# A two-layer decoder trunk: weight buffers split into three pools, and feed-forward inputs scaled before their norm is known

## The chip, the cores and the metric

The kernel runs on one core of one Trainium2 chip. The metric is the time of the whole program in device microseconds (us), from launch to the last output; lower is better. The engines that matter are TensorE (PE in the profile, with its weight loads as PEld), VectorE (DVE), ScalarE (ACT), GpSimd (POOL) and SyncE (SP), which issues the loads of the weights. Each engine works off its own instructions in the order in which they were written for it; a scheduler chose that order when the program was built.

## What is computed

Two decoder layers over 256 tokens of width 2048, in float32. Each layer has a mixer (attention of several kinds, not touched by the change) and a gated feed-forward block of width 5632, with a norm before and after each:

```python
def rms_norm(x, w):
    y = x * rsqrt(mean(x * x, axis=-1) + 1e-6)
    return y * w
...
for layer in range(2):
    u = rms_norm(h, mix_norm_pre[layer])
    u = mixer(u)                                  # two input maps, attention, output map w_out
    h = h + rms_norm(u, mix_norm_post[layer])
    u = rms_norm(h, ffn_norm_pre[layer])
    u = (silu(u @ w_gate[layer]) * (u @ w_up[layer])) @ w_down[layer]
    h = h + rms_norm(u, ffn_norm_post[layer])
```

## The kernel before, in words

The 256 tokens are two tiles of 128 rows, t = 0 and t = 1. The program has six phases in a row: input map with attention, output map and feed-forward block of layer 0, then the same three of layer 1. A phase is a list of chunks (512 output columns each), and a chunk is a list of steps. A step loads one piece of weights, 256 rows by 512 columns (512 KB), and runs its matmuls for both token tiles.

Float32 accuracy comes from splitting. `split` writes a rounded part with ACT (line 222) and the remainder with DVE (line 223); each product is then three matmuls (lines 280 to 282 in an ordinary step, 304 to 306 in a fast one). Activations are split the same way after a transpose (line 384 makes the four transposes of a 128x512 tile).

In the feed-forward block most gate and up chunks are fast chunks (`FastChunk`): five ordinary steps, then three fast steps, which multiply 2x2 blocks with seven products in place of eight. A fast step needs four sums of weight blocks, which DVE forms from the loaded piece in three instructions (lines 266, 267, 268: `split_sums`), before one ACT and one DVE instruction split seven blocks at once (128x1792). Activations need sums of their own, made once per block in `sums_of_tiles`. The order of chunks is gate 0, up 0, gate 1, up 1, gate 2, then four down chunks, then again four fast chunks (up 2, gate 3, up 3, gate 4), four down chunks, and so on. So twelve fast steps follow each other with twenty ordinary ones between them; the texts call that a burst.

Weights live in one list of 13 places of 128x2048 (`self.wp`, 8 KB per partition each). An ordinary step takes one place for its two split parts and half a place for the loaded piece; a fast step takes two places for the parts and one for the loaded piece with its sums. `load_until` records loads ahead of the matmuls. It takes the place that has been free longest, whatever it held last, and stops when too few places are free (`SPARE` = 3, in feed-forward phases `SPARE_FFN` = 5). A transfer into a place waits, on the queue of SP, until whatever last used the place is done: a split on DVE, or matmuls on PE.

At the end of the output map (`end_out`), `post_residual` does the following for each token tile. The sum of squares of the map's output gives a factor `prf` (`rms`: one DVE instruction, a power on POOL, two more on DVE); four instructions add the scaled output to x (line 466); four ACT squares of the new x (line 446) and a second `rms` give the factor `pr` of the next norm (line 416); four instructions multiply x by `pr` and the norm's weights (line 479); then come the transposes and splits that the first feed-forward matmuls read. Tile 1 runs eight steps behind tile 0 near such a boundary, so its last matmuls run while tile 0 goes through this. At the end of the feed-forward block (`end_ffn`) the weighted x is transposed without the factor, which is multiplied in later, where the attention reads its results.

## Time and profile before

| what | value |
|---|---|
| median of 3 runs (range) | 2485.02 us (2480.92 to 2485.55) |
| profiled execution: time / span | 2482.63 us / 2480.9 us |
| mean granted clock of TensorE, of full speed | 0.985 |
| busy: PE / DVE / ACT / POOL | 2395.2 / 1752.4 / 1222.8 / 206.2 us |
| moved from memory | 453.67 MB, mean 183 GB/s |

The span is from the first to the last instruction of the profiled execution; what lies around it is 1.7 us. A busy PE counts overlapping matmuls once, so the span less the busy time is time in which PE did nothing. The granted clock falls to half (1.2 of 2.4 GHz) for a while after some pauses of PE; a share of 0.83 over 10 us means that it stood at half for a third of them.

### The profile page before, as it was taken

The page shows a single profiled execution, that of the slowest core. Times are in us where ns is not written, and L with a number is a line of the kernel's source. Part 1 is how long each engine was busy: PE and PEld are TensorE (multiplying, and loading weights), DVE is VectorE, ACT ScalarE, POOL GpSimd, SP SyncE. Part 2 cuts the span into 40 slices and gives each one's busy share as a digit, 9 for nine tenths or more (in the row PEclk, how much of TensorE's full clock was granted, in tenths as well). Part 3 has the DMA queues.
Part 4 walks back from the last instruction along what each step waited for, and adds up shares of the span by engine and source line. Part 5 has one row for each costly group of instructions (what it writes and reads, how often), then busy time and mean ns, then how long its engine had stood idle before and what let it go on. Part 6 is the DMA issues. An engine that isn't in the chain of part 4 may idle for free.

```text
span 2480.9 us, 32443 instructions
## 1 busy us (share of the span) xinstructions
PE 2395.2 (97%) x12235; PEld 2005.1 (81%) x12235; DVE 1752.4 (71%) x2669; ACT 1222.8 (49%) x1833; POOL 206.2 (8%) x265
## 2 busy tenths in 40 slices
PE   9999999899999999999999999999999999999998
PEld 7878877778888887888877888887878888888876
DVE  7865775577868787778776555566776868687775
ACT  6654563454545444445455544454454535444443
POOL 0330360200000000000121000101000000000011
PEclk9999999999999999999999999999999999999999
DMA  6533434454545645555575444554464645555563
GB/s 235 196 136 136 153 136 149 152 192 163 199 165 187 212 162 197 185 212 178 204 259 186 160 168 181 206 205 166 158 229 161 215 156 204 186 186 180 189 245 126
DMA packets 131133, 453.67 MB, mean 183 GB/s; under 512 B 15568, under 2 KB 20944, under 8 KB 130976
## 3 DMA queue, kind: packets, MB, share of 16 engines
q1 hardware_dynamic: 120704, 423.81, 48.5%
q0 software_dynamic: 8112, 26.52, 3.3%
q8 instruction: 96, 1.57, 0.3%
q10 hardware_dynamic: 2160, 1.27, 0.2%
q14 instruction: 61, 0.50, 0.1%
HBM read 443.11 MB, written 8.42 MB: 182 GB/s over the span
## 4 chain that ended last, share of the span: by engine, by line
PE 65%; DVE 8%; DMA 8%; ACT 3%; issue 2%; POOL 0%; SPq 0%; DVEq 0%; POOLq 0%; ACTq 0%
PE acc L280 9%; PE p L281 9%; PE p L282 9%; PE p L280 9%; PE acc L281 9%; PE acc L282 9%; DVE w L223 4%; DMA w<-in_ffn_w_gate 4%; DMA w<-in_ffn_w_up 3%; ACT w L222 2%; PE acc L305 1%; PE acc L306 1%; PE p L305 1%; PE acc L304 1%; PE p L306 1%
## 5 line engine op out<-in xcount | busy, mean ns | idle before, releaser
L223 DVE TENSOR_TENSOR w<-w,w 128x512 fp32r<-128x512 f32 (+3 forms) x1104 | 1112.7, 1040 | 482.1 <-ACT w L222 479.7
L222 ACT ACTIVATE w<-w 128x512 fp32r<-128x512 f32 (+3 forms) x1104 | 944.4, 892 | 929.0 <-DVE w L268 287.6
L280 PE MATMUL acc<-w,m 128*128 128x512 f32 (+2 forms) x1582 | 622.3, 396 | 16.3 <-ACT w L222 9.0
L281 PE MATMUL acc<-w,m 128*128 128x512 f32 (+2 forms) x1582 | 622.0, 394 | 0.0
L282 PE MATMUL acc<-w,m 128*128 128x512 f32 (+2 forms) x1582 | 621.5, 394 | 0.2 <-DVE m L226 0.2
L280 PE MATMUL p<-w,m 128*128 128x512 f32 x1146 | 454.2, 399 | 10.7 <-ACT w L222 8.7
L281 PE MATMUL p<-w,m 128*128 128x512 f32 x1146 | 455.3, 397 | 0.9 <-DVE w L223 0.8
L282 PE MATMUL p<-w,m 128*128 128x512 f32 x1146 | 454.9, 398 | 0.0
L280 PEld LDWEIGHTS acc<-w,m 128*128 128x128 f32 x1582 | 299.5, 190 | 82.5 <-ACT w L222 10.2
L282 PEld LDWEIGHTS acc<-w,m 128*128 128x128 f32 x1582 | 298.8, 189 | 66.6 <-DVE m L226 0.6
L281 PEld LDWEIGHTS acc<-w,m 128*128 128x128 f32 x1582 | 299.0, 189 | 65.6 <-DVE w L223 0.6
L280 PEld LDWEIGHTS p<-w,m 128*128 128x128 f32 x1146 | 216.0, 189 | 60.7 <-ACT w L222 10.7
L281 PEld LDWEIGHTS p<-w,m 128*128 128x128 f32 x1146 | 216.0, 188 | 51.2 <-DVE w L223 2.4
L282 PEld LDWEIGHTS p<-w,m 128*128 128x128 f32 x1146 | 216.0, 189 | 49.8 <-DVE m L223 0.2
L266 DVE TENSOR_TENSOR w<-w 128x512 f32<-128x512 f32 x126 | 86.8, 689 | 91.0 <-DMA w<-in_ffn_w_up 54.8
L305 PE MATMUL acc<-w,m 128*128 128x256 f32 x462 | 130.9, 285 | 5.3 <-DVE w L223 5.3
L304 PE MATMUL acc<-w,m 128*128 128x256 f32 x462 | 128.1, 284 | 6.8 <-ACT w L222 6.7
L306 PE MATMUL acc<-w,m 128*128 128x256 f32 x462 | 130.3, 284 | 0.0
L433 POOL DMA_DIRECT2D m<-in_ffn_norm_post x16 | 8.8, 551 | 1342.0 <-PE acc L282 663.1
L305 PE MATMUL p<-w,m 128*128 128x256 f32 x420 | 118.3, 284 | 1.3 <-DVE w L223 1.3
L306 PE MATMUL p<-w,m 128*128 128x256 f32 x420 | 117.7, 282 | 0.0
L304 PE MATMUL p<-w,m 128*128 128x256 f32 x420 | 114.4, 282 | 3.0 <-ACT w L222 3.0
(268 smaller groups left out, 2115.3 us busy)
## 6 DMA issues: line engine op xcount, KB each, us to landing
w<-in_ffn_w_gate SPq DMA_DIRECT2D x176, 512.0 KB, 4.1
w<-in_ffn_w_up SPq DMA_DIRECT2D x176, 512.0 KB, 3.8
w<-in_ffn_w_down SPq DMA_DIRECT2D x176, 512.0 KB, 4.7
w<-in_ev_w_in SPq DMA_DIRECT2D x104, 512.0 KB, 4.4
w<-in_od_w_in SPq DMA_DIRECT2D x96, 512.0 KB, 4.3
w<-in_ev_w_out SPq DMA_DIRECT2D x32, 512.0 KB, 4.6
w<-in_od_w_out SPq DMA_DIRECT2D x32, 512.0 KB, 4.5
xd<-m POOLq DMA_DIRECT2D x24, 256.0 KB, 4.1
```

The lines of the kernel that those rows point to most:

```text
L222: self.nc.scalar.activation(h, src, AF.Copy)
L223: self.nc.vector.tensor_sub(l, src, h.bitcast(F32))
L266: nc.vector.tensor_sub(b[:, 4:6], b[:, 0:1].broadcast_to([P, 2, 256]), b[:, 1:3])
L280: nc.tensor.matmul(acc, xh, s.wh[:, j], start=(s.first and j == 0), stop=False)
L281: nc.tensor.matmul(acc, xh, s.wl[:, j], start=False, stop=False)
L282: nc.tensor.matmul(acc, xl, s.wh[:, j], start=False, stop=end)
L304: nc.tensor.matmul(acc, xh, s.wh[:, b], start=s.first and i in (0, 2), stop=True, **kw)
L305: nc.tensor.matmul(acc, xh, s.wl[:, b], start=False, stop=True, **kw)
L306: nc.tensor.matmul(acc, xl, s.wh[:, b], start=False, stop=True, **kw)
L433: self.nc.gpsimd.dma_start(out=w, in_=src.broadcast_to([P, 512]))
```

## The change

The 13 places become three pools of the same total size: `WB` = 10 buffers for split weights (`wpool`, 80 KB per partition), `RAW` = 4 for loaded pieces (`rpool`, 16 KB) and two for the sums (`spool`, 8 KB). Each pool hands out its buffers in turn. Loads are recorded ahead as long as the steps from the current one on need no more than ten buffers. The seven blocks of a fast step are split in two parts: three blocks straight from the loaded piece, four from the sums.

The input of the feed-forward block is multiplied by a number that is known before the residual is added: `scale`, the inverse root of the sum of the mean square of x before the mixer (`v`, kept from the earlier norm) and the mean square of three quarters of the mixer's post-norm weights. The true factor divided by `scale` (`r`) is multiplied in later: by ACT in the silu, by DVE in the product of gate and up. `prenorm_factor` now runs after `post_residual` at both kinds of boundary, at ordinary priority, in `end_out` behind the activation sums too.

```diff
-        wpool = pool("w", bufs=1)
+        self.wpool = pool("w", bufs=WB)
+        self.rpool = pool("raw", bufs=RAW)
+        self.spool = pool("sums", bufs=2)
...
     def load_until(self, n, end=None):
...
-            if len(self.wp.free) < need + (self.spare - 1 - held if self.loaded > n else 0):
+            if sum(a.places for a in self.steps[n:self.loaded + 1]) > WB:
                 break
-            s.w = [self.wp.pop(1) for i in range(s.places)]
+            raw = self.rpool.tile([P, 1024], F32, name="raw", tag="raw")
+            w = [self.wpool.tile([P, 2048], F32R, name="w", tag="w") for i in range(s.places)]
...
     def split_sums(self, b, s, wh, wl):
-        nc.vector.tensor_sub(b[:, 4:6], b[:, 0:1].broadcast_to([P, 2, 256]), b[:, 1:3])
-        nc.vector.tensor_sub(b[:, 6], b[:, 1], b[:, 5])
-        nc.vector.tensor_sub(b[:, 7], b[:, 3], b[:, 6])
...
-        self.split(s.wh, s.wl, b[:, 1:8])
+        t = self.spool.tile([P, 1024], F32, name="sums", tag="sums").rearrange("p (b n) -> p b n", b=4)
+        nc.vector.tensor_sub(t[:, 0:2], b[:, 0:1].broadcast_to([P, 2, 256]), b[:, 1:3])
+        nc.vector.tensor_sub(t[:, 2], b[:, 1], t[:, 1])
+        nc.vector.tensor_sub(t[:, 3], b[:, 3], t[:, 2])
+        self.split(s.wh[:, :3], s.wl[:, :3], b[:, 1:4])
+        self.split(s.wh[:, 3:], s.wl[:, 3:], t)
...
-    def prenorm_factor(self, t):
+    def prenorm_factor(self, t, scaled=False):
...
+        if scaled:
+            self.nc.vector.scalar_tensor_tensor(self.r[t], y, f, self.unscale[t], op0=ALU.mult, op1=ALU.mult)
+        else:
+            self.nc.vector.tensor_mul(self.r[t], y, f)
...
+    def next_scale(self, t):
+        nc = self.nc
+        a, j, b = self.t("psa", [P, 1]), self.t("psj", [P, 3]), self.t("psb", [P, 1])
+        nc.vector.tensor_scalar(j, self.wss[:, :3], 1.0 / 1536, 0.0, op0=ALU.mult, op1=ALU.add, accum_out=a)
+        nc.vector.tensor_add(b, a, self.v[t])
+        y, f = self.rsqrt(b, 1, "ps")
+        self.scale[t], self.unscale[t] = self.t("pscale", [P, 1]), self.t("punscale", [P, 1])
+        nc.vector.tensor_mul(self.scale[t], y, f)
+        nc.vector.tensor_mul(self.unscale[t], b, self.scale[t])
...
+            elif then == "ffn":
+                nc.vector.scalar_tensor_tensor(y, x, self.scale[t], self.nwb[c], op0=ALU.mult, op1=ALU.mult)
+                self.aT[t].append(self.transposed(y))
...
-        if then != "out":
-            self.prenorm_factor(t)
-        if then == "ffn":
-            for c in range(4):
-                y = self.y[t][c]
-                nc.vector.scalar_tensor_tensor(y, self.x[t][c], self.r[t], self.nwb[c], op0=ALU.mult, op1=ALU.mult)
-                self.aT[t].append(self.transposed(y))
...
     def gate_fast(self, out):
-            self.nc.scalar.activation(a, a, AF.Silu)
+            self.nc.scalar.activation(a, a, AF.Silu, scale=self.r[t])
...
     def up_fast(self, f, out):
-            self.nc.vector.tensor_mul(u, out[t], u)
+            self.nc.vector.scalar_tensor_tensor(u, out[t], self.r[t], u, op0=ALU.mult, op1=ALU.mult)
...
     def out_chunk(self, t, layer, c, acc):
         self.norm_weight(y, "mix_norm_post", layer, c)
+        if t == 0:
+            if c == 0:
+                self.wss = self.t("wss", [P, 4], 2)
+            self.square_sum(y, self.wss[:, c:c + 1])
+        if c == 2:
+            self.next_scale(t)
...
     def end_out(self, t, layer):
         with self.tc.high_priority(offset=LEAD):
             self.post_residual(t, "ffn")
+        if t == 1:
+            self.sums_of_tiles(self.y)
+            for b in range(2):
+                self.mem.give(*self.y[b])
+        self.prenorm_factor(t, True)
```

The change moves instructions on every engine. Three places are shown, each as the built programs have it; line numbers of the changed program are its own. The first is the queue of SP in the feed-forward block of layer 0, where the loads of up 1 and gate 2 are issued; in brackets stand the semaphores that a row waits for (DMAHW: an earlier transfer; DVE, PE, Activation: that engine). Before:

```order
L247 DMA w_5538<-in_ffn_w_up 128x1024 [waits DMAHW6_49,DMAHW3_49,DVE_49]
L247 DMA w_5538<-in_ffn_w_up 128x1024
L257 DMA w_5662<-in_ffn_w_up 128x1024 [waits PE_49]
L257 DMA w_5629<-in_ffn_w_up 128x1024 [waits PE_49]
L257 DMA w_5606<-in_ffn_w_up 128x1024 [waits DMAHW4_49,DMAHW7_49,DMAHW3_49,DVE_49]
L247 DMA w_5698<-in_ffn_w_gate 128x1024 [waits DMAHW0_49,PE_49]
L247 DMA w_5698<-in_ffn_w_gate 128x1024 [waits DMAHW1_49]
L247 DMA w_5730<-in_ffn_w_gate 128x1024 [waits DMAHW2_49,PE_49]
L247 DMA w_5730<-in_ffn_w_gate 128x1024
```

And in the changed program:

```order
L248 DMA raw<-in_ffn_w_up 128x1024 [waits DMAHW0_49,DVE_49]
L248 DMA raw<-in_ffn_w_up 128x1024 [waits DMAHW1_49,DVE_49]
L248 DMA raw<-in_ffn_w_up 128x1024 [waits DMAHW2_49,DVE_49]
L241 DMA raw<-in_ffn_w_gate 128x1024 [waits DMAHW3_49,DVE_49]
L241 DMA raw<-in_ffn_w_gate 128x1024 [waits DMAHW4_49,DVE_49]
L241 DMA raw<-in_ffn_w_gate 128x1024 [waits DMAHW5_49,DVE_49,Activation_49]
L241 DMA raw<-in_ffn_w_gate 128x1024 [waits DMAHW7_49,DVE_49]
L241 DMA raw<-in_ffn_w_gate 128x1024 [waits DMAHW6_49,DVE_49]
```

Of the 808 loads of weights, 372 wait for PE before; in the changed program none does, and they come in the order of the steps.

The second place is ACT in the same burst: the splits of up 1's fast steps (`128x1792` before; `raw 128x768` and `sums 128x1024` now) among ordinary ones. Before:

```order
L222 ACTIVATE w_5660<-w_5662 128x1792 [waits DMAHW5_49,DVE_49,PE_49]
L686 ACTIVATE m_5594<-m_5594 128x512 [waits DVE_49]
L222 ACTIVATE w_5697<-w_5698 128x1024 [waits DMAHW0_49,PE_49]
L222 ACTIVATE w_5627<-w_5629 128x1792 [waits DMAHW6_49,DVE_49]
L222 ACTIVATE w_5604<-w_5606 128x1792 [waits DMAHW7_49,DVE_49]
L222 ACTIVATE w_5734<-w_5730 128x1024 [waits DMAHW3_49,PE_49]
L222 ACTIVATE w_5669<-w_5568 128x1024 [waits DMAHW2_49,DVE_49]
L222 ACTIVATE w_5729<-w_5730 128x1024 [waits DMAHW2_49,DVE_49]
L222 ACTIVATE w_5702<-w_5698 128x1024 [waits DMAHW1_49,DVE_49]
```

And in the changed program, where L301 is the chunk's first read of its results (L310 before) and L683 the silu (L686 before):

```order
L221 ACTIVATE w<-raw 128x768 [waits DMAHW4_49,PE_49,Activation_49]
L221 ACTIVATE w<-raw 128x768 [waits DMAHW5_49,PE_49,Activation_49]
L301 ACTIVATE m_5753<-p_5671 128x256 [waits PE_49]
L221 ACTIVATE w<-sums 128x1024 [waits DVE_49]
L221 ACTIVATE w<-raw 128x768 [waits DMAHW6_49,PE_49,Activation_49]
L221 ACTIVATE w<-sums 128x1024 [waits DVE_49]
L221 ACTIVATE w<-raw 128x1024 [waits DMAHW7_49,PE_49]
L683 ACTIVATE m_5753<-m_5753,pr 128x512 [waits DVE_49,Activation_49]
L221 ACTIVATE w<-raw 128x1024 [waits DMAHW0_49,PE_49]
L683 ACTIVATE m_5754<-m_5754,pr 128x512 [waits DVE_49]
L221 ACTIVATE w<-sums 128x1024 [waits DVE_49]
```

The wait for PE has moved from the load to the split. Before, two pieces of the next chunk (w_5697, w_5734) stand ahead of pieces that PE needs sooner (w_5604, w_5669); now the loaded pieces stand in the order of the steps, and the part from the sums follows a few rows behind.

The third place is DVE at the end of layer 0's output map, token tile 0: residual, factor and scaled input. Before (L466 residual, L416 the factor `pr`, L479 the scaled input, L223 remainders of weight splits):

```order
L466 SCALAR_TENSOR_TENSOR m_4260<-m_4788,prf,m_4260 128x512
L206 TENSOR_SCALAR pj,pv<-xss 128x5
L223 TENSOR_TENSOR w_4903<-w_4904,w_4903 128x512 x2
L223 TENSOR_TENSOR w_4916<-w_4904,w_4916 128x512
L195 SCALAR_TENSOR_TENSOR pna<-pny,pv 128x1
L223 TENSOR_TENSOR w_4916<-w_4904,w_4916 128x512
L199 TENSOR_SCALAR pna<-pna 128x1
L416 TENSOR_TENSOR pr<-pny,pna 128x1
L479 SCALAR_TENSOR_TENSOR m_4273<-m_4257,pr,m_4265 128x512
L479 SCALAR_TENSOR_TENSOR m_4506<-m_4258,pr,m_4266 128x512
L479 SCALAR_TENSOR_TENSOR m_4679<-m_4259,pr,m_4267 128x512
L479 SCALAR_TENSOR_TENSOR m_4788<-m_4260,pr,m_4268 128x512
```

And in the changed program (L471 residual, L478 the scaled input, L222 remainders of weight splits):

```order
L471 SCALAR_TENSOR_TENSOR m_4328<-m_4344,prf,m_4328 128x512
L471 SCALAR_TENSOR_TENSOR m_4329<-m_4585,prf,m_4329 128x512
L471 SCALAR_TENSOR_TENSOR m_4330<-m_4765,prf,m_4330 128x512
L471 SCALAR_TENSOR_TENSOR m_4331<-m_4906,prf,m_4331 128x512
L222 TENSOR_TENSOR w<-raw,w 128x512 x2
L478 SCALAR_TENSOR_TENSOR m_4344<-m_4328,pscale,m_4336 128x512
L222 TENSOR_TENSOR w<-raw,w 128x512
L478 SCALAR_TENSOR_TENSOR m_4585<-m_4329,pscale,m_4337 128x512
L478 SCALAR_TENSOR_TENSOR m_4765<-m_4330,pscale,m_4338 128x512
L222 TENSOR_TENSOR w<-raw,w 128x512
L478 SCALAR_TENSOR_TENSOR m_4906<-m_4331,pscale,m_4339 128x512
L222 TENSOR_TENSOR w<-raw,w 128x512 x3
```

Between the residual and the scaled input stood a chain of sum, power and product; now two remainders of weight splits stand there, and two more between the four scaled tiles. On PE the transposes of tile 0 stand behind tile 1's last matmul in both programs.

## Rows read from the trace of the kernel before

**Rows 1.** Page, part 1: engine, busy us (share) x instructions.

```profile
PE 2395.2 (97%) x12235; PEld 2005.1 (81%) x12235; DVE 1752.4 (71%) x2669; ACT 1222.8 (49%) x1833; POOL 206.2 (8%) x265
```

**Rows 2.** Windows, both feed-forward layers: length, busy us, PEclk, DMA share, GB/s.

```profile
549.00:1290.00 741.00, 727.35 (x3807) 614.94 (x3806) 561.94 (x694) 354.50 (x360) 17.57 (x29) 0.99 0.54 189
1715.00:2470.00 755.00, 736.50 (x3846) 621.37 (x3844) 561.71 (x698) 346.48 (x357) 19.63 (x28) 0.99 0.53 185
```

**Rows 3.** Waits on PE, layer 0: total us, times, longest us.

```profile
PE acc L280 <- ACT w L222: 6.5, 4, 2.5
PE p L304 <- ACT w L222: 2.8, 2, 2.5
```

**Rows 4.** Waits on PE, layer 1.

```profile
PE acc L305 <- DVE w L223: 5.3, 4, 1.3
```

**Rows 5.** Windows of 10 us, after a wait and in the open.

```profile
636.00:646.00 10.00, 8.54 (x61) 8.29 (x61) 9.27 (x8) 3.98 (x5) 0.00 (x0) 0.83 0.28 91
700.00:710.00 10.00, 10.00 (x45) 8.05 (x44) 4.29 (x5) 3.76 (x4) 0.00 (x0) 1.00 0.18 55
```

**Rows 6.** Waits of the SP queue, layer 0.

```profile
SPq L247 <- PE p L282: 125.1, 39, 7.6
...
SPq L257 <- PE p L282: 62.8, 14, 8.0
```

**Rows 7.** Waits on DVE, layer 0.

```profile
DVE w L223 <- ACT w L222: 115.1, 106, 3.3
DVE w L266 <- DMA w<-in_ffn_w_gate: 29.6, 17, 3.3
```

**Rows 8.** Lines by form, DVE, layer 0: busy, mean, idle before.

```profile
L223 DVE TENSOR_TENSOR w<-w,w 128x1024 fp32r<-128x1024 f32 x193 | 232.2, 1222 | 83.8 <-ACT w L222 83.1
L223 DVE TENSOR_TENSOR w<-w,w 128x1792 fp32r<-128x1792 f32 x63 | 127.3, 2021 | 30.7 <-ACT w L222 30.7
```

**Rows 9.** The same, ACT.

```profile
L222 ACT ACTIVATE w<-w 128x1024 fp32r<-128x1024 f32 x193 | 200.2, 1058 | 160.6 <-DMA w<-in_ffn_w_down 61.1 <-DVE w L223 41.3 <-DMA w<-in_ffn_w_up 35.1
L222 ACT ACTIVATE w<-w 128x1792 fp32r<-128x1792 f32 x63 | 106.7, 1700 | 129.6 <-DVE w L268 129.6
```

**Rows 10.** Windows around the three boundaries between phases.

```profile
540.00:560.00 20.00, 16.83 (x71) 12.94 (x70) 17.79 (x34) 12.47 (x24) 2.80 (x6) 0.91 0.57 220
1700.00:1725.00 25.00, 19.32 (x84) 15.70 (x83) 19.26 (x42) 13.64 (x27) 3.92 (x8) 0.93 0.51 196
1296.00:1316.00 20.00, 14.35 (x59) 10.94 (x58) 20.00 (x38) 14.49 (x32) 8.83 (x10) 0.83 0.57 226
```

**Rows 11.** Waits on PE, boundary of layer 1.

```profile
PE acc L384 <- DVE m L479: 4.5, 1, 4.5
```

**Rows 12.** Timeline of DVE there: start us, us, what.

```profile
1695.34 2.74 DVE L466 SCALAR_TENSOR_TENSOR m<-m,prf,m 128x512 f32<-128x512 f32 x4
...
1705.81 1.29 DVE L223 TENSOR_TENSOR w<-w,w 128x512 fp32r<-128x512 f32 x2 [3.13 <-ACT w L222]
1707.02 0.15 DVE L416 TENSOR_TENSOR pr<-pny,pna 128x1 f32<-128x1 f32 x1
```

**Rows 13.** Timeline of PE there.

```profile
1703.86 0.40 PE L282 MATMUL p<-w,m 128*128 128x512 f32 x1
1708.77 1.51 PE L384 MATMUL acc<-ident,m 128*128 128x128 f32 x6 [4.52 <-DVE m L479]
```

**Rows 14.** Lines of the whole span, four operations.

```profile
L446 ACT ACTIVATE m<-m 128x512 f32<-128x512 f32 x48 | 30.3, 632 | 41.6 <-DVE m L725 21.9 <-DVE m L466 12.2 <-DVE prf L463 4.3
...
L479 DVE SCALAR_TENSOR_TENSOR m<-m,pr,m 128x512 f32<-128x512 f32 x16 | 11.0, 747 | 0.1
L796 ACT ACTIVATE m<-p,pr 128x512 f32<-128x512 f32 x16 | 10.8, 677 | 8.1 <-PE p L282 8.1
...
L722 ACT ACTIVATE m<-p 128x512 f32<-128x512 f32 x8 | 4.7, 588 | 4.4 <-PE p L282 4.4
```

**Rows 15.** Windows, a burst of layer 1.

```profile
1770.00:1830.00 60.00, 51.51 (x288) 43.22 (x286) 48.69 (x64) 31.09 (x30) 0.00 (x0) 0.99 0.50 176
```

More of the change, by code (lines that the diff above doesn't have):

```diff
@@ L45 @@
 WB = 10
-WPLACES = 13
-SPARE = 3
-SPARE_FFN = 5
+RAW = 4
 LAG_FFN = 1
@@ L156, in __init__ @@
         self.mem = Pool(big, "m", NTILES)
-        self.wp = Pool(wpool, "w", WPLACES, (P, 2048))
-        self.spare, self.lag, self.half = SPARE, LAG, None
+        self.lag = LAG
         self.ps = Pool(psb, "p", NPS)
@@ L166, in __init__ @@
         self.S = None
-        self.x, self.y, self.yss, self.aT, self.r = ([None] * 2 for _ in range(5))
+        self.x, self.y, self.yss, self.aT, self.r, self.v, self.scale, self.unscale = ([None] * 2 for _ in range(8))
         self.mix = [{}, {}]
@@ L202, in rms @@
     def rms(self, ss):
-        v = self.t("pv", [P, 1])
+        v = self.t("pv", [P, 1], 8)
         j = self.t("pj", [P, 5])
         self.nc.vector.tensor_scalar(j, ss, 1.0 / D, 0.0, op0=ALU.mult, op1=ALU.add, accum_out=v)
-        return self.rsqrt(v, 1, "pn")
+        return self.rsqrt(v, 1, "pn") + (v,)
     def sums(self):
@@ L233, in load_until @@
             s = self.steps[self.loaded]
-            held = self.half is not None
-            need = s.places + (not held or s.pair is not None)
-            if len(self.wp.free) < need + (self.spare - 1 - held if self.loaded > n else 0):
+            if sum(a.places for a in self.steps[n:self.loaded + 1]) > WB:
                 break
-            s.w = [self.wp.pop(1) for i in range(s.places)]
-            w = [a.bitcast(F32R) for a in s.w]
+            raw = self.rpool.tile([P, 1024], F32, name="raw", tag="raw")
+            w = [self.wpool.tile([P, 2048], F32R, name="w", tag="w") for i in range(s.places)]
             if s.pair is None:
                 n_ = s.src.shape[2]
-                done = self.half
-                self.half = done or self.wp.pop(1)
-                raw = self.half[:, 1024:] if done else self.half[:, :1024]
                 raw, s.wh, s.wl = (a.rearrange("p (k n) -> p k n", k=2)[:, :, :n_]
@@ L252, in load_until @@
                         self.split(s.wh[:, j], s.wl[:, j], raw[:, j])
-                if done:
-                    self.half = None
-            else:
-                done = self.wp.pop(1)
-                nc.sync.dma_start(out=done[:, :1024], in_=s.src.rearrange("p k n -> p (k n)"))
-                self.split_sums(done.rearrange("p (b n) -> p b n", b=8), s, *w)
-            if done:
-                self.wp.give(done)
+            else:
+                nc.sync.dma_start(out=raw, in_=s.src.rearrange("p k n -> p (k n)"))
+                self.split_sums(raw.rearrange("p (b n) -> p b n", b=4), s, *w)
             self.loaded += 1
@@ L345, in run_phase @@
                     self.fast_step(self.steps[n0])
-                    self.wp.give(*self.steps[n1].w)
                     n0 += 1
@@ L358, in run_phase @@
                 self.step(1, self.steps[n1])
-                self.wp.give(*self.steps[n1].w)
                 n1 += 1
@@ L413, in prenorm_factor @@
             self.square_sum(self.x[t][c], ss[:, c:c + 1])
-        y, f = self.rms(ss)
+        y, f, self.v[t] = self.rms(ss)
         self.r[t] = self.t("pr", [P, 1])
-        self.nc.vector.tensor_mul(self.r[t], y, f)
+        if scaled:
[11 more added lines that the diff above has]
+        nc.vector.tensor_mul(self.unscale[t], b, self.scale[t])
     def free_S(self):
@@ L460, in post_residual @@
         self.aT[t] = []
-        r, f = self.rms(self.yss[t])
+        r, f, v = self.rms(self.yss[t])
         rf = self.t("prf", [P, 1])
@@ L471, in post_residual @@
                 self.aT[t].append(self.transposed(y))
+            elif then == "ffn":
+                nc.vector.scalar_tensor_tensor(y, x, self.scale[t], self.nwb[c], op0=ALU.mult, op1=ALU.mult)
+                self.aT[t].append(self.transposed(y))
             if then != "ffn":
                 self.mem.give(y)
-        if then != "out":
-            self.prenorm_factor(t)
-        if then == "ffn":
-            for c in range(4):
-                y = self.y[t][c]
-                nc.vector.scalar_tensor_tensor(y, self.x[t][c], self.r[t], self.nwb[c], op0=ALU.mult, op1=ALU.mult)
-                self.aT[t].append(self.transposed(y))
-            if t == 1:
-                self.sums_of_tiles(self.y)
-                for b in range(2):
-                    self.mem.give(*self.y[b])
         if t == 1 and then != "out":
@@ L536, in run @@
                     self.mem.give(self.mask)
-                self.spare, self.lag = SPARE_FFN, LAG_FFN
+                self.lag = LAG_FFN
             self.run_phase(lo, hi, end)
-            self.spare, self.lag = SPARE, LAG
+            self.lag = LAG
             if i % 3 == 2:
@@ L680, in gate_chunk @@
         self.sg[t] = self.now(self.mem)
-        self.nc.scalar.activation(self.sg[t], acc, AF.Silu)
+        self.nc.scalar.activation(self.sg[t], acc, AF.Silu, scale=self.r[t])
     def gate_fast(self, out):
         self.sg = out
-        for a in out:
-            self.nc.scalar.activation(a, a, AF.Silu)
+        for t, a in enumerate(out):
+            self.nc.scalar.activation(a, a, AF.Silu, scale=self.r[t])
     def up_fast(self, f, out):
@@ L741, in end_ffn @@
         if layer == 0:
+            self.prenorm_factor(t)
             self.store_x(t)
```

## The prediction

> **What bounds the kernel now.** I read the page first. PE is busy for 2395.2 of 2480.9 us [rows 1], so the most that any rearrangement can save is 85.7 us of idle time plus what the lowered clock costs; every other engine has room. A change pays only where PE stands still, so the next view is the list of waits on PE, stage by stage. The two feed-forward blocks hold 741.00 - 727.35 = 13.7 us and 755.00 - 736.50 = 18.5 us of idle PE [rows 2]. There PE waits for nothing but the splits of weights: for the rounded part (L222 on ACT) or the remainder (L223 on DVE), with single waits of up to 2.5 us [rows 3, 4]. The reader should see that these are late weights, not late activations.
>
> The three boundaries that the change touches come next. Around them PE is idle for 3.2, 5.7 and 5.7 us [rows 10]. What is left of the 85.7 us, some 39 us, lies in attention, at the start and at the end, which the change does not aim at.
>
> Each longer wait is paid for twice. After one the granted clock is 0.83 over 10 us, where it is 1.00 in the open [rows 5]; that is a third of the stretch at 1.2 GHz, and it costs 10 x 0.17 = 1.7 us of full-speed work. I find eight such stretches in the two feed-forward blocks.
>
> **Term 1, the weight pools.** Before, a load waits on SP's queue for the last user of its place, mostly a matmul [rows 6]. The split of the piece can begin only when the transfer has landed, so the transfer lies in series between a place that comes free and weights that are ready. DVE and ACT feel it: in layer 0 DVE stands 29.6 us for gate pieces ahead of the sums (L266) and 115.1 us for ACT [rows 7], and ACT stands 129.6 us for DVE's sums [rows 9]. With the pools, a load waits only for the split four pieces earlier, and four pieces can lie in memory ahead of the splits. What waits for PE is now the split itself, on ACT's queue; behind it stand the chunk's first read of its results and the silu, as the second excerpt shows. The first of these needs the same matmuls to be finished anyway, so I charge nothing for it. If ACT were held there longer, PE would wait for the new split in place of the old one, which is the second rival.
>
> What this removes at most is all the idle time of the blocks and their eight slow stretches: 13.7 + 18.5 + 8 x 1.7 = 45.8 us. At least it removes nothing. I take three quarters, 34 us. The longest waits follow directly on late transfers, and the most regular one (L305, four waits of 1.3 us [rows 4]) comes from a remainder of 1792 columns that takes 2021 ns [rows 8] and is now cut, so that the block which PE needs first is ready sooner. But DVE is busy for 48.69 of 60 us in the hardest burst [rows 15], and some of its lateness is work, not waiting; hence not all.
>
> **Term 2, what the pools add.** The split of seven blocks becomes two. From 1024 to 1792 columns DVE goes from 1222 to 2021 ns [rows 8], 1.04 ns a column, so 768 columns cost 956 ns and the pair 2178 ns, 157 ns more. On ACT the same working (1058 and 1700 ns, 0.836 a column [rows 9]) gives 844 + 1058 - 1700 = 202 ns more. There are 126 fast steps: 20 us of DVE and 25 us of ACT over the program. In layer 0's block DVE has 741.00 - 561.94 = 179 us free and ACT 386 us [rows 2], so I count this at nothing; without that cover it is the first rival.
>
> At the start the ring of four is new. The fifth load must wait for the first split, where before it found an empty place. The first matmuls wait for activations then too. Nothing in the trace shows this wait; it lies between 0 and the 2 us that four transfers could slip, and I take 2 us.
>
> **Term 3, the boundary before the feed-forward block.** In layer 1 tile 0's residual starts at 1695.34 and ends at 1698.08; the factor `pr` comes out only at 1707.02, after four squares, a second power and a DVE that stood 3.13 us for ACT [rows 12]. PE finished tile 1's work at 1704.26 and began the transposes at 1708.77, a wait of 4.5 us for L479 [rows 11, 13]. With the known scale nothing stands between residual and scaled tile but weight remainders. From the third excerpt: four residuals (2.74 us), four scaled tiles (747 ns each [rows 14], at most 2.99 us) and four remainders of 512 columns, each at most 1222 - 512 x 1.04 = 0.69 us, so 2.8 us. The last tile is ready at 1695.34 + 8.5 = 1703.9, the first two tiles well before; PE arrives at 1704.26. The wait for L479 goes, and the slow stretch behind it most likely too. The margin is thin for the last tile, and if DVE stands for ACT once it is gone, but then PE can still begin with the first.
>
> Idle and slow time together are 3.2 + 20 x 0.09 = 5.0 us at layer 0 and 5.7 + 25 x 0.07 = 7.4 us at layer 1 [rows 10], 12.4 us. The transposes still stand behind tile 1's last matmul, so PE still has to see one split go through ACT: I keep 1.9 us for the two layers and take 10.5 us. Bounds are 0 and 12.4.
>
> What is added off this path: eight squares of norm weights on ACT (632 ns each [rows 14]), four short chains with a power, a scale from memory in the silu (677 against 588 ns [rows 14], 44 times, 4 us) and a three-operand product in place of a two-operand one (747 against about 690 ns, 44 times, 2.5 us). On POOL the deferred factor's power stands among the stores of x; the first silu that needs it comes eight steps later. All lie in blocks where both engines have the room named above. One square stands just ahead of tile 0's last product with the norm weights; its 0.6 us is inside the 1.9 us kept.
>
> **Term 4, the boundary after the feed-forward block.** The squares and the power there lose their high priority. The boundary costs 5.7 + 20 x 0.17 = 9.1 us [rows 10], of which the late weights are a part and the first transposes another that stays. I take 3 us; bounds 0 and 9.1.
>
> **Sum.** 34 - 2 + 10.5 + 3 = 45.5 us. Against the profiled execution, 2482.6 us, that gives 2437 us. That execution lies 2.4 us under the median of the three runs, so for a median I write 2440 us. The likeliest case by itself spans 2424 to 2456 us (term 1 between 50% and all but a few us).
>
> **Rivals.** First, slower: DVE becomes the bound in the bursts. It leaves 60.0 - 48.69 = 11.3 us unused in one [rows 15], and if that is order and latency that can't be filled, the 157 ns more of each of twelve fast steps add 1.9 us to every burst. There are five full bursts a layer, ten in all: 19 us more, less terms 3, 4 and the start (11.5), so 7.5 us slower, 2492 us. It decides when a burst's usable gap on DVE falls below 1.9 us. For it speaks that DVE's waits for ACT (L223) outweigh its waits for transfers [rows 7]; against it that ACT's own waits are for the sums and for transfers [rows 9], both of which begin earlier.
>
> Second: the feed-forward waits stay as they are, since the split buffers still come free at PE's pace and the earlier transfers only wait longer in memory. Then only the boundaries count: 2482.6 - 11.5, as a median 2474 us. For it speaks that a fast step still holds two buffers, so a burst's lead is five fast steps; against it the 372 loads that no longer wait for PE.
>
> Third: all of it goes, in the blocks and at the boundaries: 45.8 + 12.4 + 9.1 = 67 us, 2418 us as a median. It needs the waits to be a matter of room alone. The Trainium skill (Perfetto Trace Analysis, Identifying Performance Opportunities) says that the same gap, repeating over a stretch on the engine that should be saturated, can mean too few buffers for the next tile. The four equal waits of 1.3 us agree with the pattern; by that rule all of term 1 would go.
>
> Fourth: nothing measurable. The scheduler wrote the order of every engine anew, and attention holds idle time enough for a new order to lose what the blocks gain: within 5 us of 2485.
>
> **How the numbers follow.** Chances: the forecast 0.48, all of it 0.12, boundaries alone 0.17, nothing 0.08, DVE-bound 0.15. Faster by over 0.2% (5 us, about what a measurement of this kernel can tell from no change) is the first three, 0.77; the same 0.08; slower 0.15. The range runs from 2412 us (all of it, and 6 us of attention besides) to 2488 us, short of the slower rival's centre; what is left outside is some 0.03 below and 0.12 above.
>
> **What would show it.** Waits of the loads for PE gone from SP's list; idle PE of at most 4 us in each feed-forward block and a granted clock of 1.00 through most of it; DVE's waits for transfers at L257 near zero; at both output boundaries the first transpose within 1 us of tile 1's last matmul. It is wrong if DVE is busy without pause in the bursts and PE still waits for the remainder (first rival), if the waits on PE in the blocks are the old ones with transfers landed early (second), or if idle time in attention grows by more than a few us.

## The result, and the profile after

The change makes the kernel faster: 2393.65 us (median of 4 runs, 2393.09 to 2395.03) against 2484.78 us for the kernel before (median of 4 runs), a ratio of 0.9637 with a 95% interval of 0.962 to 0.9654. That is 91 us, where 45 were forecast; the time lies below the range.

Page, part 1, of the changed kernel, which answers to [rows 1]:

```profile
PE 2346.8 (98%) x12235; PEld 2007.9 (84%) x12235; DVE 1760.4 (74%) x2823; ACT 1256.2 (52%) x1975; POOL 218.6 (9%) x269
```

The span is 2393.3 us, 87.6 less than before. Idle time on PE fell from 85.7 to 46.5 us, which explains 39. The other 48 us went out of the *busy* time of an engine that runs the same 12235 matmuls. Some 13 of them are the granted clock, a mean of 0.990 after 0.985 (2480.9 x 0.015 less 2393.3 x 0.010). The reader should stop at the remaining 35: a busy engine with the same work at the same clock ought to be busy for the same time.

The windows of the two feed-forward blocks, which answer to [rows 2] (length, then busy us of PE, PEld, DVE, ACT and POOL, PEclk, DMA share, GB/s); the first still holds a boundary at each end:

```profile
540.00:1275.00 735.00, 726.84 (x3866) 627.01 (x3865) 585.33 (x798) 379.39 (x461) 33.12 (x47) 0.99 0.61 201
1690.00:2380.00 690.00, 690.00 (x3710) 598.73 (x3709) 541.38 (x714) 349.11 (x397) 15.63 (x23) 1.00 0.60 196
```

Layer 1's block has no idle time at all, and its clock is 1.00. The waits of [rows 3, 4] are gone. What is left on the list of PE's waits (total us, times, longest) lies in attention and at the boundaries (the second row is the one behind layer 0's block):

```profile
PE p L1175 <- POOL m L1160: 9.3, 2, 6.0
PE p L373 <- DVE m L475: 4.9, 1, 4.9
PE acc L271 <- ACT m L224: 3.2, 2, 2.6
```

Waits of the SP queue between 540 and 1275 us, which answer to [rows 6]: no load waits for PE any more, they wait for the splits and sums that last read their place.

```profile
SPq L241 <- DVE w L222: 327.2, 142, 12.0
SPq L248 <- DVE w L222: 119.5, 53, 4.0
SPq L241 <- DVE sums L259: 95.4, 33, 7.5
```

Lines by form in the same window, DVE and then ACT, which answer to [rows 8, 9] (busy us, mean ns, idle before and what ended it):

```profile
L222 DVE TENSOR_TENSOR w<-sums,w 128x1024 fp32r<-128x1024 f32 x63 | 76.7, 1218 | 1.6 <-ACT w L221 1.5
L222 DVE TENSOR_TENSOR w<-raw,w 128x768 fp32r<-128x768 f32 x63 | 60.0, 952 | 23.6 <-PE p L273 15.5 <-PE acc L273 6.0 <-ACT w L221 2.1
```

```profile
L221 ACT ACTIVATE w<-sums 128x1024 fp32r<-128x1024 f32 x63 | 66.1, 1050 | 7.9 <-DVE sums L259 7.8
L221 ACT ACTIVATE w<-raw 128x768 fp32r<-128x768 f32 x63 | 53.0, 841 | 48.6 <-issue 26.4 <-PE acc L273 5.3 <-PE p L297 4.3
```

ACT's wait for DVE's sums fell from 129.6 us [rows 9] to 7.8.

The three boundaries, which answer to [rows 10]: PE is idle for 1.6 and 2.2 us ahead of the feed-forward blocks (3.2 and 5.7 before) and for 4.6 us behind the first (5.7 before), where the clock is lower than it was (0.74 after 0.83).

```profile
530.00:550.00 20.00, 18.42 (x87) 14.96 (x86) 19.42 (x44) 10.03 (x21) 3.78 (x8) 0.91 0.64 211
1650.00:1675.00 25.00, 22.84 (x107) 18.24 (x106) 24.49 (x49) 14.10 (x32) 5.96 (x11) 1.00 0.76 252
1260.00:1280.00 20.00, 15.38 (x62) 12.19 (x63) 17.79 (x41) 7.79 (x19) 9.67 (x11) 0.74 0.62 212
```

Where did PE's busy time go? Take 50 us in which it does nothing but 128x512 matmuls, the down chunks of layer 0, first in the kernel before (1075 to 1125 us) and then after. Columns: length, PE's busy us and matmuls, PEclk, DMA share, GB/s.

```profile
1075.00:1125.00 50.00, 50.00 (x216) 1.00 0.56 200
```

```profile
1040.00:1090.00 50.00, 50.00 (x222) 1.00 0.59 191
```

Both are busy without a gap at a granted clock of 1.00, but 222 matmuls fit where 216 did. From their starts in the whole trace, the median distance between two of them is 233 ns before and 227 ns after; there are 8008. The 256-column matmuls of the fast steps (2646) went the other way, from 114 to 120 ns.

### The profile page after: what moved, and what is told of

It is laid out like the page before. It is cut to its first block, busy times and chain, and to the rows that moved or that the text cites. A ratio compares the mean times of both kernels' runs of the same rounds, so it can differ in the third digit from the quotient of the medians.

```text
span 2393.3 us, 33293 instructions
## 1 busy us (share of the span) xinstructions
PE 2346.8 (98%) x12235; PEld 2007.9 (84%) x12235; DVE 1760.4 (74%) x2823; ACT 1256.2 (52%) x1975; POOL 218.6 (9%) x269
## 4 chain that ended last, share of the span: by engine, by line
PE 80%; DVE 3%; DMA 1%; issue 1%; POOL 1%; ACT 1%; DVEq 0%; POOLq 0%; ACTq 0%
PE p L273 11%; PE p L271 11%; PE p L272 11%; PE acc L273 10%; PE acc L271 10%; PE acc L272 10%; PE acc L296 2%; PE acc L297 2%; PE acc L295 2%; PE p L297 2%; PE p L296 2%; PE p L295 2%; DVE w L222 1%; PE p L216 1%; DMA raw<-in_ffn_w_down 1%
## 5 line engine op out<-in xcount | busy, mean ns | idle before, releaser
L222 DVE TENSOR_TENSOR w<-raw,w 128x512 fp32r<-128x512 f32 (+4 forms) x1104 | 987.2, 915 | 432.6 <-ACT w L221 386.6
L221 ACT ACTIVATE w<-raw 128x512 fp32r<-128x512 f32 (+4 forms) x1104 | 844.1, 795 | 832.5 <-PE p L273 313.7
L271 PE MATMUL p<-w,m 128*128 128x512 f32 x1146 | 450.0, 393 | 3.6 <-ACT m L221 2.9
L273 PE MATMUL p<-w,m 128*128 128x512 f32 x1146 | 449.9, 393 | 0.0
L272 PE MATMUL p<-w,m 128*128 128x512 f32 x1146 | 449.3, 392 | 0.0
L222 DVE TENSOR_TENSOR w<-sums,w 128x1024 fp32r<-128x1024 f32 x126 | 153.5, 1218 | 3.0 <-ACT w L221 2.9
L221 ACT ACTIVATE w<-sums 128x1024 fp32r<-128x1024 f32 x126 | 132.4, 1051 | 18.8 <-DVE sums L259 18.5
L257 DVE TENSOR_TENSOR sums<-raw 128x512 f32<-128x512 f32 x126 | 86.8, 689 | 51.1 <-DMA raw<-in_ffn_w_gate 25.4
L297 PE MATMUL p<-w,m 128*128 128x256 f32 x420 | 119.3, 284 | 0.0
```

What stands on the lines that cost most here:

```text
L221: self.nc.scalar.activation(h, src, AF.Copy)
L222: self.nc.vector.tensor_sub(l, src, h.bitcast(F32))
L257: nc.vector.tensor_sub(t[:, 0:2], b[:, 0:1].broadcast_to([P, 2, 256]), b[:, 1:3])
L271: nc.tensor.matmul(acc, xh, s.wh[:, j], start=(s.first and j == 0), stop=False)
L272: nc.tensor.matmul(acc, xh, s.wl[:, j], start=False, stop=False)
L273: nc.tensor.matmul(acc, xl, s.wh[:, j], start=False, stop=end)
```

## The experiments

My first theory was that the pitch of the matmuls hangs on where their operands lie in memory. The small tiles that the change adds (`psa`, `pscale` and others) take 960 bytes a partition, and the pool of activation tiles m begins behind them: at byte 133568 before and 134528 after, as the built programs list them. The split weights w begin at 23424 in both. The rivals: the separate buffers, or the moved norms.

**The place of m, and each half of the change by itself.** Four kernels. The first is the kernel before with the line below; the second is the change with the same line and 16 columns in place of 240. The others hold the hunks on the pools, or those on the norms and `scale`, alone.

```diff
+        self.tmp.tile([P, 240], F32, name="pad", tag="pad")
```

> The kernel before with one unused tile of 960 bytes a partition in the pool of small tiles, so that the activation tiles m (matmul's stationary operand) begin at byte 134528 of a partition, where the change puts them, and no longer at 133568; w stays at 23424. Same instructions in the same order. Two things in the result ask for a cause: the idle time on PE that went (85.7 to 46.5 us), and the pitch of back-to-back 128x512 matmuls, which fell from 0.2335 to 0.2275 us in every stage, 8008 of them. Address theory: the pitch hangs on where the stationary tiles lie; this kernel runs them at 0.2275 us, its waits stay as they were, and it takes 2485 - 35 to 46, so 2439 to 2450 us. Buffer theory: the pitch fell since split weights and loaded pieces no longer share places; this kernel has the old buffers and stays at 2485 us and 0.2335 us. Third theory, the instructions of the norm (other reads and writes beside the matmuls) set it: 2485 us too.

> The changed kernel with one unused tile of 64 bytes a partition, so that the tiles m begin at byte 134592, which stands to 128 bytes as in the kernel before (64 over), and not at 134528 (a multiple of 128). Address theory: pitch back at 0.2335 us with no PE wait in the feed-forward blocks, 2394 + 35 to 46 = 2429 to 2440 us, which is the time that was forecast. Buffer theory and norm theory: 2394 us, 0.2275 us.

> The separate weight pools alone, norms as before; the tiles m stay at byte 133568. Address theory: only the waits in the feed-forward blocks and their slow stretches go: 2485 - 34 to 46 = 2439 to 2451 us, pitch 0.2335 us. Buffer theory: the pitch falls as well, 2395 to 2405 us. Norm theory: as the address theory for this kernel.

> The known scale and the moved norms alone, weights in one list as before; its small tiles push m to byte 134528. Address theory: pitch 0.2275 us, so 35 to 46 us, and 5 to 15 us at the boundaries: 2424 to 2445 us, with the weight waits in the feed-forward blocks as before. Buffer theory: boundaries alone, 2470 to 2480 us, pitch 0.2335 us. Norm theory: as the address theory for this kernel.

| kernel | median us | ratio to before (95%) | median pitch, 512 / 256 columns |
|---|---|---|---|
| before, m moved | 2457.52 | 0.9888 (0.9863 to 0.9914) | 227 / 120 ns |
| after, m moved | 2415.86 | 0.9721 (0.9694 to 0.9748) | 233 / 114 ns |
| pools only | 2426.13 | 0.9764 (0.974 to 0.9787) | 233 / 114 ns |
| scale only | 2457.84 | 0.9892 (0.9863 to 0.992) | 227 / 120 ns |

The place of m alone sets the pitch, with either set of buffers and either norm. Windows of 50 us with nothing but 512-column matmuls, of the kernel before with m moved and of the change with m moved:

```profile
1065.00:1115.00 50.00, 50.00 (x222) 1.00 0.62 220
```

```profile
1050.00:1100.00 50.00, 50.00 (x216) 1.00 0.57 182
```

It is worth 28 us in the kernel before (1 - 0.9888) and 21 in the change (0.9721 - 0.9637), less than the 35 to 46 expected: 8008 x 6 ns is 48 us, but the fast matmuls give back 2646 x 6 ns, 16 us, so 32 were to be expected. I had counted one kind of matmul only. The rest is the difference between medians and means: where the clock is full, the mean distance falls by 4.8 ns with 512 columns and rises by 3.8 (before) and 4.8 ns (change) with 256, which gives 28 and 26 us.

The pools alone gave 59 us (0.0236 x 2484) with the pitch unchanged, more than my bound. Where this comes from is seen in one block, from its first fast matmul to its last. Timeline of PE (start us, us, what) in the kernel before, and with the pools alone:

```profile
589.30 0.28 PE L304 MATMUL p<-w,m 128*128 128x256 f32 x1
...
1235.55 0.29 PE L306 MATMUL p<-w,m 128*128 128x256 f32 x1
```

```profile
582.35 0.28 PE L295 MATMUL p<-w,m 128*128 128x256 f32 x1
...
1200.38 0.28 PE L297 MATMUL p<-w,m 128*128 128x256 f32 x1
```

646.2 us became 618.0, in a block whose windows showed 13.7 us of idle time [rows 2]. Of these 28 us 3 are work that moved: fourteen matmuls of 512 columns fewer lie between the two marks (3370 in place of 3384 matmuls). I counted, over both blocks, what each distance between two starts exceeds the median for its width: 50.8 us before, 1.7 with the pools, so 49 of the 59 us. The other 10 lie outside the blocks (7 by the spans of the two profiled executions). Of the 50.8, 29.2 are idle time, 11.7 lie in slow stretches and 10 are stalls that no view calls idle. One of these, in the kernel before:

```profile
1804.89 0.28 PE L306 MATMUL acc<-w,m 128*128 128x256 f32 x1
...
1805.28 0.39 PE L304 MATMUL acc<-w,m 128*128 128x256 f32 x1
```

The second starts 0.39 us after the first, where 0.12 is the rule. But a matmul lasts 0.28 us from its start to its modelled end, so 0.16 of the 0.27 us lost counts as busy.

The scale alone, against the kernel before with m at the same byte, gave nothing (0.9892 and 0.9888): PE idles 83.1 us and not 86.1 (span less busy time), but the granted clock is 0.983 and not 0.985, which takes back 5. On top of the pools it gave 11 us (0.9764 - 0.9721, some 8 us either way); there PE idles 47.5 us after 50.3, and the clock is 0.991 after 0.988, which is 7 us. The waits show what happened. Waits on PE with the pools alone: at both boundaries ahead of the feed-forward blocks the transposes wait for the scaled tile (L468).

```profile
PE p L373 <- DVE m L459: 4.7, 1, 4.7
PE acc L373 <- DVE m L468: 4.7, 1, 4.7
PE p L373 <- DVE m L468: 4.1, 1, 4.1
```

In the changed kernel both waits for the scaled tile are gone. DVE's timeline ahead of layer 1's block, which answers to [rows 12], and PE's, which answers to [rows 13]:

```profile
1649.35 2.73 DVE L471 SCALAR_TENSOR_TENSOR m<-m,prf,m 128x512 f32<-128x512 f32 x4
...
1656.39 0.75 DVE L478 SCALAR_TENSOR_TENSOR m<-m,pscale,m 128x512 f32<-128x512 f32 x1
...
1667.76 0.21 DVE L407 SCALAR_TENSOR_TENSOR pr<-pny,pna,punscale 128x1 f32<-128x1 f32 x1
```

```profile
1660.61 0.50 PE L271 MATMUL acc<-w,m 128*128 128x512 f32 x1 [1.20 <-ACT m L221]
```

The last scaled tile is done 7.8 us after the residual begins; the factor `pr` comes some 11 us later, and PE doesn't wait for it. The first of the three waits above, behind layer 0's feed-forward block, is as long in the change (L475).

**Which relation of the operands counts.** The change once more, with m or w shifted by unused tiles in `tmp` or ahead of everything in `const`.

> The changed kernel with the split weights w (matmul's moving operand) 64 bytes past a multiple of 128 and the tiles m (the stationary one) on a multiple of 128, by two unused tiles of 64 bytes. Stationary theory: only where m lies counts; 0.227 us a matmul of 512 columns and 2394 us. Relative theory: the two operands have to stand alike to 128 bytes; here they don't, 0.233 us and 2416 us. Moving theory: either operand off the multiple costs as much; 2416 us or more.

> The changed kernel with w and m both 64 bytes past a multiple of 128, by one unused tile of 64 bytes ahead of everything. Stationary theory: 0.233 us and 2416 us. Relative theory: they stand alike, 0.227 us and 2394 us. Moving theory: 2416 us or more.

> The changed kernel with m 32 bytes past a multiple of 128 and w on a multiple, by one unused tile of 32 bytes. If a multiple of 128 is what counts, this is as slow as the 64 (2416 us, 0.233 us); if 32 bytes are enough, 2394 us; if the finer the offset the worse, above 2420 us.

> The changed kernel with w and m both on multiples of 512 bytes, by one unused tile of 128 bytes ahead of everything (before this both were 384 past one). If only the remainder to 128 counts: 2394 us, the same. If larger multiples help too: pitch under 0.226 us, and at 0.220 us some 45 us less, 2350 us.

> The changed kernel with m 96 bytes past a multiple of 128 and w on one, by one unused tile of 96 bytes. By the relative theory a difference other than 0 costs: as for 32 (2426 us; 0.233 us for 512 columns, 0.118 for 256) or for 64 (2416 us; 0.233 and 0.114). If only 32 and 64 cost, 2394 us.

| w and m past a multiple of 128 bytes | difference | median us | median pitch, 512 / 256 columns |
|---|---|---|---|
| 0 and 0 (the change) | 0 | 2393.65 | 227 / 120 ns |
| 64 and 64 | 0 | 2394.32 | 227 / 120 ns |
| 0 and 0 (both on multiples of 512) | 0 | 2394.64 | 227 / 120 ns |
| 0 and 64 | 64 | 2415.86 | 233 / 114 ns |
| 64 and 0 | 64 | 2415.86 | not read |
| 0 and 32 | 32 | 2426.35 | 233 / 118 ns |
| 0 and 96 | 96 | 2430.67 | 234 / 118 ns |

Neither operand's own address counts, the difference does. The relative theory holds, and the two others fall. Both operands on multiples of 512 give nothing more. That 32 and 96 are slower than 64 comes from the fast matmuls: 2646 x 4 ns is 10.6 us, and 2426.35 less 2415.86 is 10.5. One thing stays open: in all the runs with difference 0 the two operands differ by a whole multiple of 512 bytes, so that a difference of 128 or 256 would do as well is not shown.

**Each kind of matmul at its better difference.** The 512-column ones are best at 0 and the fast ones at 64. A fast step's two buffers have room for the shift:

```diff
-        s.wh, s.wl = (a.rearrange("p (b n) -> p b n", b=8)[:, :7] for a in (wh, wl))
+        s.wh, s.wl = (a[:, 16:16 + 7 * 256].rearrange("p (b n) -> p b n", b=7) for a in (wh, wl))
```

> The changed kernel with the seven blocks of a fast step's split weights begun 64 bytes (16 columns) later inside their two buffers, so that the 2646 fast matmuls of 256 columns read moving and stationary operands that differ by 64 to 128 bytes, and the 512-column ones still read operands that stand alike. By the relative theory a fast matmul goes from 0.120 to 0.114 us (as where all differed by 64), the others stay at 0.227: 2646 x 0.006 = 16 us less, 2378 us. If the relation of whole tiles counted and not that of the bytes read, or if the fast pitch came from something else: 2394 us.

2384.76 us, a ratio of 0.9608 (0.9588 to 0.9627), the fastest version here, and it beats both kernels. Timeline of PE, two matmuls 24 apart at the start of a fast step, in the change and here: 2.88 us against 2.72, so 120 and 113 ns.

```profile
1095.27 0.28 PE L295 MATMUL acc<-w,m 128*128 128x256 f32 x1
...
1098.15 0.28 PE L295 MATMUL acc<-w,m 128*128 128x256 f32 x1
```

```profile
1091.08 0.28 PE L295 MATMUL acc<-w,m 128*128 128x256 f32 x1
...
1093.80 0.28 PE L295 MATMUL acc<-w,m 128*128 128x256 f32 x1
```

The bytes that are read count, not where a tile begins. It gained some 9 us and not 16, most likely since the mean pitch fell by less than the median (from 120.3 to 115.9 ns in the blocks, 12 us).

**The cut of the split, and the number of places.** The changed kernel with the seven blocks split in one piece and the sums beside the loaded piece (8 KB each, three of them); with two and three places at the cut as it is; with five, and one for the sums; and with eight split buffers and eight places (`WB = 8`, `RAW = 8`).

```diff
-RAW = 4
+RAW = 3
...
-        self.split(s.wh[:, :3], s.wl[:, :3], b[:, 1:4])
-        self.split(s.wh[:, 3:], s.wl[:, 3:], t)
+        self.split(s.wh, s.wl, b[:, 1:8])
```

> The changed kernel with the seven blocks split in one piece again (1792 columns), the sums beside the loaded piece in a buffer of 8 KB, of which three fit in the same memory; m at the same byte as in the change. The forecast's reason for the regular waits (a remainder of 1792 columns comes too late): five waits of 1.3 us a layer come back, each with some slow clock behind it, 8 to 20 us, 2402 to 2414 us. If only the room for weights counted: 2394 us, or less by what DVE and ACT save (157 and 202 ns a fast step, all hidden).

> The changed kernel with two places for loaded pieces in place of four (m moves by a multiple of 128 bytes). Lead theory: the gain in the feed-forward blocks comes from pieces that lie landed ahead of the splits, so with two the transfer stands between split and split again; waits of PE come back in the blocks, 2405 to 2440 us. Place theory: it is enough that a load waits for a split and not for a matmul, and that all ten split buffers are the splits' own; 2394 to 2400 us.

> The changed kernel with three places for loaded pieces, the split cut in two as in the change: against the run that split in one piece it differs by the cut alone. If the number of pieces ahead is what counts, it loses like that run, 2460 to 2490 us; if the cut is what counts, 2394 to 2405 us.

> The changed kernel with five places for loaded pieces and one for the sums in place of four and two, in the same memory. If pieces ahead still count at four, the waits left in attention shrink and it takes 2375 to 2390 us; if four are enough, 2394 us, and more if the single place for the sums holds DVE up.

> The changed kernel with eight buffers for split weights and eight places for loaded pieces in place of ten and four, in the same memory. If the loaded pieces are what counts, at most 2394 us; if the split buffers count too (a fast step holds two of them, so four steps of lead in place of five), PE waits for splits in the feed-forward blocks again, 2410 to 2450 us.

| kernel | median us | ratio (95%) |
|---|---|---|
| not cut, three places | 2482.97 | 0.9993 (0.9977 to 1.0009) |
| two places | 2706.06 | 1.0904 (1.0881 to 1.0927) |
| three places | 2415.98 | 0.9729 (0.9709 to 0.9748) |
| five places, one for the sums | 2395.95 | 0.9646 (0.9625 to 0.9666) |
| eight buffers, eight places | 2403.82 | 0.9679 (0.9661 to 0.9697) |

The run without the cut and the one with two places took far longer than expected, and three places lie between the two forecasts. At three places the cut decides between three quarters of the change's gain and none of it: 66 us (63 of them in the two blocks, from the first fast matmul to the last), of which a part may be that without the cut a loaded piece, which then lies in one place with its sums, gives its place back later. PE's waits without the cut (first fence: the products of gate and up come late, twenty times) and with two places (second fence):

```profile
PE p L215 <- DVE m L689: 39.2, 20, 4.6
...
PE acc L293 <- DVE w L221: 8.4, 4, 3.1
```

```profile
PE acc L295 <- ACT w L221: 38.9, 69, 1.9
PE acc L272 <- DVE w L222: 25.6, 55, 1.1
```

With two places a transfer (a median of 3.4 to 3.5 us from issue to landing) stands between the splits again: ACT stands for the landing of a feed-forward piece 472 times, in the change 57 times. Three cost 23 us, all but some 2 of them outside the feed-forward blocks, five give no more than four, and eight of each lose 10 us, all outside the blocks, where PE did not wait for splits as expected. So four is just enough, and the 2 us that the prediction set down for the ring hold for four alone. The fastest version with five places ran as well:

> The changed kernel with the fast steps' blocks 64 bytes later (2384.8 us by itself) and five places for loaded pieces with one for the sums. If both gains add up, 2385 less what the fifth place gives: 2365 to 2385 us; 2385 us if four places were enough.

2385.26 us, 0.9606 (0.9584 to 0.9627): the fifth place adds nothing there either.

**The cut alone, and the sum.** The kernel before with the one instruction of the diff above made two, its list of places untouched; and the pools alone with m at byte 134528.

> The kernel before with the seven blocks split in two parts (three from the loaded piece, four from the sums) and nothing else changed: one list of places, m where it was. If the cut by itself removes the regular waits for a late remainder: 2465 to 2478 us. If the cut gives nothing without the separate places (a load still waits for matmuls): 2485 us, or up to 5 us more by the longer splits on DVE and ACT (157 and 202 ns a fast step).

> The separate weight pools alone, with an unused tile of 960 bytes that puts m at byte 134528 as in the change. If the three parts add up (58 us for the pools, 24 for the place of m, 10 for the boundaries): 2426 - 24 = 2402 us, 8 to 10 us over the change. If the boundaries are worth nothing there: 2394 us.

The cut by itself gives 2443.05 us, 0.9853 (0.9826 to 0.988): 37 us, with no buffer added and loads that still wait for PE. That is more than either theory gave it. Lines by form, ACT, between 549 and 1290 us, in that kernel:

```profile
L222 ACT ACTIVATE w<-w 128x1024 fp32r<-128x1024 f32 x255 | 263.2, 1056 | 220.5 <-DVE w L268 64.1 <-DMA w<-in_ffn_w_down 53.4 <-DMA w<-in_ffn_w_up 41.5
L222 ACT ACTIVATE w<-w 128x768 fp32r<-128x768 f32 x63 | 53.3, 847 | 93.8 <-DMA w<-in_ffn_w_up 51.7 <-DMA w<-in_ffn_w_gate 39.4 <-DVE w L223 2.5
```

ACT stands for DVE's sums for 64.1 us where it stood for 129.6 [rows 9]: it rounds the three loaded blocks while DVE still forms the sums. DVE's remainder of 1792 columns hung behind both, 1.7 us on ACT and 2.0 on DVE in series. By the count over starts the stalls of the two blocks are 14 us here, where they were 50.8 before and 1.7 with the pools. So the cut's 37 us lie in the blocks, and of what the separate places add about 12 lie there.

The pools with m moved take 2403.12 us, 0.9681 (0.9664 to 0.9699), where 2402 was to be expected if the parts add up. So the change can be read as a path in this order, in steps between ratios times 2484 us: the cut 37, the separate places with their rule for loads 22, the place of m 21, the known scale 11, each good to some 6 to 9 us. The scale's step is the same with m at either place (0.0043 and 0.0044).

## Why the prediction was wrong

The direction was right, and the waits that terms 1 and 3 aimed at did go; the size was half.

**The bound failed first.** "The most that any rearrangement can save is 85.7 us of idle time plus what the lowered clock costs" took busy time at full clock for work that no rearrangement can shorten. As a sum it was not passed (85.7 and some 37 us of lowered clock are more than 91), but what was saved came in part from elsewhere: 21 us from a pitch that the change set by accident, through the bytes of its small tiles, and 10 us from stalls hidden inside modelled matmul lengths. The terms, which were sized from idle and slow time alone, could reach 67 us at most (the third rival). Both could be seen: the first in 216 matmuls where 50 us of 1.00 clock hold 222, though not without a kernel to compare; the second by taking distances between starts instead of idle time.

**Term 1 (34 us, bound 45.8): measured 59.** The waits and slow stretches all went (41 us of the 50.8 in the blocks), so "three quarters" was too careful. Above the bound lay the hidden stalls and some 10 us outside the blocks, for which the prediction had no term. The reason was misplaced as well: I put the gain down to transfers that no longer wait for PE and gave the cut a place at the end. Measured, the cut is 37 of the 59 and the places 22. The third rival's rule (the Trainium skill, Perfetto Trace Analysis, Identifying Performance Opportunities: repeated equal gaps can mean too little room for the next tile) pointed at the right waits, and the regular gaps went. But the cut removed most of them without any room added, so in this kernel they were mainly the latency of a serial split.

**Term 2: right in its costs.** The two parts take 952 + 1218 = 2170 ns on DVE (2178 forecast) and 841 + 1050 = 1891 on ACT (1902), and nothing of it showed in PE's waits in the blocks. The first rival, a DVE that becomes the bound, did not come: DVE is busy for 541.38 of 690 us in layer 1's block and PE never waits there. The 2 us at the start did not show.

**Term 3 (10.5 us): measured 11,** some 8 us either way, so that the two agree so closely is partly luck. The last scaled tile came 7.8 us after the residual's start where 8.5 were worked out. One condition was missing: without the pools it is worth nothing (2457.84 against 2457.52 us), so it is no separate term. There the idle time fell by 3 us and the clock took it back; which pauses lowered the clock was not settled.

**Term 4 (3 us): nothing.** Idle and slow time at this boundary are 4.6 + 20 x 0.26 = 9.8 us, where they were 9.1. The transposes behind layer 0's feed-forward block wait 4.9 us for the residual times the norm's weights (L475), and the first matmul 2.9 us more for the first split. The factor was not what they waited for.

The second rival is out, as no wait in the blocks is an old one; the fourth is out too. The third, "all of it goes", came closest: with m at its old remainder the change takes 2415.86 us, 69 us less than before and inside the range, where that rival had 67 and 2418. It was right that the waits in the blocks all go, though not in why; as a number it met the runs by luck, since term 4 gave nothing and the hidden stalls and the 10 us outside the blocks made up for it. One sign of the forecast did not come: DVE still stands 25.0 us for transfers ahead of the sums in layer 0's block (L257; 48.8 us at L266 before), at no cost to PE.

## What to carry to other kernels

Count matmuls per microsecond in a stretch without waits before calling a busy PE full, and sum the distances between starts, since small stalls hide inside the matmuls' modelled ends. When a change adds even a few bytes of tiles, look at where the operands of the matmuls moved, and pad to separate that from the change proper. A long two-engine operation on the way to the matmuls is worth cutting where part of its input is ready earlier, and a ring of loaded pieces has a sharp edge: here two, three and four places took 2706, 2416 and 2394 us.

## What the runs showed of the hardware that was not expected

With float32r operands the distance between back-to-back matmuls depends on the difference of the two operands' byte addresses in a partition. Beyond a multiple of 512 bytes (m less w) differences of 0, 32, 64 and 96 were run, and minus 64, which took the same time as 64. With 512 columns the distance is 227 ns at 0 and 233 to 234 at 32, 64 and 96; with 256 columns it is 120 ns at 0, 114 at 64 and 118 at 32 and 96. Weight loads beside the 512-column matmuls take 188 to 190 ns in both kernels, the splits on DVE and ACT take as long as before, and within either kernel the median pitch of the 512-column matmuls is the same whether or not DVE, ACT or the DMAs are at work at the time (233 and 227 ns). Which of PE's two reads is held up, and why the shorter matmuls like the other difference, stays open: no view shows it.
